# Squares folded on the vector engine, junk matmuls moved, and a conditioning pair loaded by half chunks, in the head of a decoder trunk

## The chip, the cores and the metric

The kernel runs on one NeuronCore of a Trainium2 chip. The metric is device time of one execution in microseconds, median over several; smaller is better. Five engines have queues of their own: TensorE (PE; its weight loads are shown as PEld), VectorE (DVE), ScalarE (ACT), GpSimd (POOL) and SyncE (SP), which issues almost all transfers.

## The reference, cut to what matters

Two layers over one sequence of 256 positions and 1024 channels, in float32. A layer is a token mixer and a squared-ReLU MLP; each is preceded by an RMSNorm that is modulated by a vector c:

```python
c_act = jax.nn.silu(c)
for i in range(DEPTH):
    mod = c_act @ w_mod[i] + b_mod[i]
    sh1, sc1, g1, sh2, sc2, g2 = jnp.split(mod, 6, axis=-1)
    h = modulate(rmsnorm(x, norm_mix[i]), sh1, sc1)     # h * (1 + sc1) + sh1
    y = pool_mixer(h, ...) if i % 2 == 0 else moba_attention(h, ...)
    x = x + g1[:, None, :] * y
    h = modulate(rmsnorm(x, norm_mlp[i]), sh2, sc2)
    x = x + g2[:, None, :] * squared_relu_mlp(h, w_up[i], w_down[i])
return rmsnorm(x, norm_final)
```

The change lies in layer 0, between the pooling mixer's output and the first matmul of the up projection.

## The kernel before

Activations lie channels by positions: `xs[k]` is block k of 128 channels (k from 0 to 7), 128x256. Weights stream in chunks of 1 MB, in the hand-written order `LOADS`, into five buffers (`RAW_BUFS`); `issue()` asks SP for the next chunk of the order each time a buffer's last use has been issued. Weights of the MLPs and projections are split into a high and a low part (ScalarE casts, L247; VectorE subtracts, L252), and each product takes three matmul passes.

The head of the program, up to about 54 us, is one order written out by hand. It computes six vectors of layer 0 as needed, each cut into four pieces of 256 channels. A "pair" is two such pieces whose weights (2 MB) come in two chunks. `pair_mm` (`take`, L313) multiplies c into one chunk, with 32 output columns in each of four quarters of the array, and `pair_out` (`given`, L324) picks each channel's value from the result and adds the bias, on VectorE. There are two layouts. Pairs in `BY_VECTOR` have a whole vector's piece in each chunk: a take is 64 passes of 64 columns, and each piece is finished after its own chunk. The other pairs have half of the summed dimension of both pieces in each chunk: a take is 32 passes of 128 columns, and both pieces are finished after the second chunk (`both_given`).

The mixer works in four groups of 256 channels, 3 to 0. `pool_out(g)` adds the gated mixer output to x (L453) for the group's two blocks, and ScalarE squares them (L528). `pool_sums` sums the squares over channels with matmuls whose moving operand is one column of ones (`sums`, L389: two matmuls of two passes each for one block). `n1.rstd()` makes the norm row r from the sums (one ScalarE step, then five on VectorE, L399 to L406), and `n1.spread()` (L410) multiplies it out to all partitions. The pair mlp0 is the scale and the shift of the MLP's norm for channels 0 to 255. `gain` (L357) joins the scale with the norm's weight. `Input.scaled` (L637) multiplies x by gain and norm on VectorE, `Input.high` (L643) adds the shift and rounds to the high part on ScalarE, `Input.low` (L646) makes the rest. Then `up` runs its 256 tiles; the first eight are done in three sweeps of eight matmuls (`mm_sums`, L279), later ones three passes at a time. The pair mlp1 is taken at tiles 13 and 20.

`keep_warm(n)` issues n matmuls of a constant tile (L342, "junk", two passes of 256 columns each) whose result nothing reads.

In the head before, mlp0's first take ran ahead of the spread and its second behind it:

```python
    take("mlp0", 0)
    given("mlp0", 0)
    ...
    R1 = n1.spread()
    take("mlp0", 1)
    ...
    first.scaled(R1)
    given("mlp0", 1)
```

Of the kernel before, what the change touches and what calls it, by code (L numbers as in the profile page):

```python
# [51 lines left out]
PAIRS |= {f"mlp{j}": ((0, 4, j), (0, 3, j)) for j in range(2)}  # L52
PAIRS["shift2"] = ((0, 3, 2),)

BY_VECTOR = {"g10", "mlp0", "shift2"}


G_UP0, G_UP1, G_QKV, G_WO = 14, 4, 4, 5
# [82 lines left out]
def tile_hybrid_pool_moba(  # L141
# [12 lines left out]
    nc = tc.nc  # L154
# [11 lines left out]
    def bank(name):  # L166
        return ps.tile([P, 512], F32, tag="ps", name=name)

    def al_tile(shape, name, dt=F32):
        return act.tile(shape, dt, tag="al", bufs=KF, name=name)  # L170
# [11 lines left out]
    def issue():  # L182
        i = n_issued[0]
        if i == len(LOADS):
            return
        n_issued[0] += 1
        key = LOADS[i]
        half = HALF * P
        if key[0] == "p":
            t = al_tile([P, 4 * P], f"wp{key[1]}")  # L190
            nc.sync.dma_start(t, w_pool[0][:, key[1] * 4 * P : (key[1] + 1) * 4 * P])
        elif key[0] == "w0a":
            t = loaded["w", 0] = raw_tile("w_0")
            nc.sync.dma_start(t[:, :half], w_all[0][:, :half])
        elif key[0] == "w0b":
            t = loaded["w", 0]
            nc.sync.dma_start(t[:, half:], w_all[0][:, half:])
        else:
            if key[0] == "c":
                layer, m, j = PAIRS[key[1]][key[2]]  # L200
                src = w_mod[layer, m * 4 + j]
            else:
                src = w_mod[key[1], key[2] * 4 + key[3]] if key[0] == "m" else w_all[key[1]]
            t = raw_tile("_".join(str(a) for a in key))
            nc.sync.dma_start(t, src)
        loaded[key] = t

        if n_issued[0] < len(LOADS) and LOADS[n_issued[0]][0] in ("p", "w0b"):
            issue()
# [7 lines left out]
    for _ in range(RAW_BUFS):  # L217
        issue()
    ident = vec[:, V_ID : V_ID + P]
    pick = vec[:, V_PICK : V_PICK + 32]  # L220
    rc = vec[:, V_RC : V_RC + 64].rearrange("p (a b) -> p a b", a=4)
    ones = const.tile([P, 1], F32, name="ones")
# [21 lines left out]
    def split_hi(h):  # L244
        raw = loaded["w", h // 2][:, h % 2 * HALF * P : (h % 2 + 1) * HALF * P]
        hi = split_p.tile([P, HALF * P], F32R, tag="whi", name=f"w{h}_hi")
        nc.scalar.copy(hi, raw)  # L247
        return raw, hi
# [56 lines left out]
    def pair_mm(name, i, region):  # L305
        whole = name in BY_VECTOR
        nk = KD if whole else KD // 2
        w = loaded["c", name, i].rearrange("p (k q n) -> p k q n", k=nk, q=4)
        cols = slice(64 * i, 64 * i + 64) if whole else slice(0, P)
        for k in range(nk):  # L310
            c0 = k if whole else i * nk + k
            for q in range(4):
                nc.tensor.matmul(  # L313
                    region[32 * q : 32 * q + 32, cols], ccol[:, c0 : c0 + 1].to_broadcast([P, 32]), w[:, k, q],
                    start=c0 == 0, stop=c0 == KD - 1, skip_group_check=True,
                )
        issue()

    def pair_out(name, i, region):
        key = PAIRS[name][i]  # L320
        layer, m, j = key
        for a in range(2):
            t = tmp.tile([P, 32], F32, tag="pk", bufs=4, name="pk")
            nc.vector.scalar_tensor_tensor(  # L324
                t, region[:, (2 * i + a) * 32 : (2 * i + a + 1) * 32], mod_bias(*key)[:, a : a + 1], pick,
                op0=ALU.add, op1=ALU.mult, accum_out=mods[layer, m][:, 2 * j + a : 2 * j + a + 1],
            )
        known.add(key)
# [11 lines left out]
    def keep_warm(n):  # L340
        for _ in range(n):
            nc.tensor.matmul(junk[0][:, :S], fill[:, :P], fill, start=True, stop=True)  # L342
# [23 lines left out]
    class Rms:  # L366
# [13 lines left out]
        def fold(self, k):  # L380
            if k > 0:
                nc.vector.tensor_add(self.acc, self.acc, self.sq.pop(k))
# [69 lines left out]
    def residual_sum(src, k, gate):  # L452
        nc.vector.scalar_tensor_tensor(xs[k], src, gate[:, k : k + 1], xs[k], op0=ALU.mult, op1=ALU.add)  # L453
# [65 lines left out]
    n1 = Rms("n1")  # L519
    sq1 = {}  # L520

    def pool_out(g):
        cols = slice(2 * g, 2 * g + 2)
        nc.vector.tensor_mul(g1[:, cols], mods[0, 2][:, cols], vec[:, V_PSC + 2 * g : V_PSC + 2 * g + 2])
        for n in range(2):
            residual_sum(pools[g][:, n * S : (n + 1) * S], 2 * g + n, g1)
            sq1[2 * g + n] = al_tile([P, S], f"n1_sq{2 * g + n}")
            nc.scalar.activation(sq1[2 * g + n], xs[2 * g + n], AF.Square)  # L528

    def pool_sums(g):  # L530
        for n in range(2):
            n1.sums(sq1[2 * g + n], (g, n) == (0, 1))

    def take(name, half):
        pair_mm(name, half, region[name])

    def given(name, i):
        pair_out(name, i, region[name])

    def both_given(name):  # L540
        for i in range(2):
            given(name, i)
# [55 lines left out]
    pool_products(0)  # L598
    both_given("g32")
    pool_out(3)  # L600
    pool_out(2)
    take("g10", 0)
    given("g10", 0)
    pool_out(1)
    pool_sums(3)
    pool_sums(2)
    take("g10", 1)
    given("g10", 1)
    pool_out(0)
    pool_sums(1)  # L610
    pool_sums(0)
    n1.rstd()
    take("mlp0", 0)
    given("mlp0", 0)
    gs01 = const.tile([P, KD], F32, name="gs0_4")
    gain(0, 4, V_NMLP, gs01, 0, 2)
    R1 = n1.spread()
    take("mlp0", 1)
    junk[0] = bank("junk2")
    keep_warm(2)  # L620

# [213 lines left out]

    first = Input(0)
    first.scaled(R1)
    given("mlp0", 1)
    w0 = split_hi(0)
    first.high()  # L840
    first.low(0)
# [172 lines left out]
    for i, (n, k) in enumerate(QKV_ORDER):  # L1014
        w = next_tile()
        p, j = divmod(n, 3)
# [149 lines left out]
```

## Time and profile before

| | |
|---|---|
| median of 3 executions | 549.41 us (549.16 to 550.0) |
| the profiled execution, its own time | 550.51 us |
| its span, first to last instruction | 548.7 us |
| mean granted TensorE clock | 0.990 |
| busy share: PE, PEld, DVE, ACT | 98%, 91%, 75%, 59% |
| moved by DMA | 140.43 MB, mean 256 GB/s |

All times in the rows are microseconds from the first instruction. The profiled execution's own time is the span and 1.8 us around it. An engine's busy time says little by itself; the chain that ended last says which work set the end, and the windows say in which stretch an engine was full. "issue" in the chain is time in which an engine waited for nothing that the profile shows.

### The profile page before, as it was taken

Reading aid. Unit: us, or ns where it says so; the run is one execution under the profiler, and the core shown is the slowest. Engines: PE = TensorE matmul, PEld = TensorE weight load, DVE = VectorE, ACT = ScalarE, POOL = GpSimd, SP = SyncE. Lnnn points to the kernel's source line nnn. Section 1 sums busy time; section 2 is a strip of 40 time slices with the busy share of each in tenths; the row PEclk is TensorE's granted clock in tenths of the full one; section 3 lists DMA queues with packets and bytes.
Section 4 is the critical chain, followed back from the end, with each engine's and each line's share of the span. In section 5 each row is a group of like instructions: output and inputs, shape, how many; then the busy total and the mean of one; then the engine's idle time right before and its main releaser. Section 6 shows DMA issues by size and latency. Waiting matters only on the chain.

```text
span 548.7 us, 11124 instructions
## 1 busy us (share of the span) xinstructions
PE 537.5 (98%) x4492; PEld 499.5 (91%) x4492; DVE 410.5 (75%) x830; ACT 323.6 (59%) x605; POOL 2.5 (0%) x18
## 2 busy tenths in 40 slices
PE   8998999999999999999999999999999999999995
PEld 7777999999988888999999899999999998888895
DVE  2865598799889889966999994777887786665541
ACT  4224335789744445546988778566997774444531
POOL 1000000000000000000000000000000000000000
PEclk9997999999999999999999999999999999999998
DMA  8999989468999988974558774353565567676002
GB/s 335 416 420 406 360 321 380 177 231 300 318 383 392 382 334 324 351 254 153 189 213 297 289 288 163 121 206 141 177 226 173 212 230 260 221 263 254 1 1 76
DMA packets 22339, 140.43 MB, mean 256 GB/s; under 512 B 2416, under 2 KB 4608, under 8 KB 5904
## 3 DMA queue, kind: packets, MB, share of 16 engines
q1 hardware_dynamic: 22048, 138.61, 67.8%
q10 hardware_dynamic: 144, 1.05, 0.5%
q8 instruction: 35, 0.57, 0.4%
q14 instruction: 16, 0.13, 0.1%
q0 software_dynamic: 96, 0.06, 0.0%
HBM read 138.64 MB, written 1.07 MB: 255 GB/s over the span
## 4 chain that ended last, share of the span: by engine, by line
PE 92%; DMA 6%; DVE 0%; issue 0%; ACT 0%; DVEq 0%; ACTq 0%
PE m1d L264 9%; PE m0d L264 9%; PE m1u L271 6%; PE m1u L272 6%; PE m1u L273 6%; PE m0u L271 5%; PE m0u L273 5%; PE m0u L272 5%; PE m1d L265 5%; PE m0d L265 5%; PE qkv L271 5%; PE qkv L272 4%; PE qkv L273 4%; DMA raw_c_sh<-in_w_mod 3%; DMA raw_c_g<-in_w_mod 2%; PE wo L271 1%
## 5 line engine op out<-in xcount | busy, mean ns | idle before, releaser
L252 DVE TENSOR_TENSOR w_lo<-raw_w,w_hi 128x1024 fp32r<-128x1024 f32 x160 | 194.6, 1223 | 59.5 <-ACT w_hi L247 57.8
L247 ACT CAST w_hi<-raw_w 128x1024 fp32r<-128x1024 f32 x160 | 166.4, 1047 | 76.6 <-PE m1d L264 25.0
L264 PE MATMUL m1d<-m1u_al,w_hi 128*128 128x512 f32 x224 | 78.7, 394 | 0.0
L264 PE MATMUL m0d<-m0u_al,w_hi 128*128 128x512 f32 x224 | 78.1, 392 | 0.0
L295 DVE SCALAR_TENSOR_TENSOR raw_m<-raw_m,cact 128x1024 f32<-128x1024 f32 x62 | 75.3, 1218 | 0.0
L271 PE MATMUL m1u<-h_raw,w_hi 128*128 128x258 f32 x256 | 72.8, 284 | 0.0
L272 PE MATMUL m1u<-h_raw,w_hi 128*128 128x256 f32 x256 | 72.6, 284 | 0.0
L273 PE MATMUL m1u<-h_raw,w_lo 128*128 128x258 f32 x256 | 72.5, 283 | 0.0
L271 PE MATMUL m0u<-h,w_hi 128*128 128x256 f32 x248 | 69.8, 282 | 0.0
L273 PE MATMUL m0u<-h,w_lo 128*128 128x256 f32 x248 | 69.7, 281 | 0.0
L272 PE MATMUL m0u<-h,w_hi 128*128 128x256 f32 x248 | 69.4, 280 | 0.0
L265 PE MATMUL m1d<-m1u_al,w_lo 128*128 128x256 f32 x224 | 63.0, 281 | 0.0
L265 PE MATMUL m0d<-m0u_al,w_lo 128*128 128x256 f32 x224 | 62.8, 280 | 0.0
L271 PE MATMUL qkv<-h_raw,w_hi 128*128 128x258 f32 x192 | 57.4, 299 | 0.0
L272 PE MATMUL qkv<-h_raw,w_hi 128*128 128x256 f32 x192 | 54.6, 284 | 0.0
L273 PE MATMUL qkv<-h_raw,w_lo 128*128 128x258 f32 x192 | 54.4, 283 | 0.0
L264 PEld LDWEIGHTS m1d<-m1u_al,w_hi 128*128 128x128 f32 x224 | 42.1, 188 | 9.9
L264 PEld LDWEIGHTS m0d<-m0u_al,w_hi 128*128 128x128 f32 x224 | 42.1, 188 | 9.5
L273 PEld LDWEIGHTS m1u<-h_raw,w_lo 128*128 128x128 f32 x256 | 48.8, 191 | 0.0
L271 PEld LDWEIGHTS m1u<-h_raw,w_hi 128*128 128x128 f32 x256 | 48.7, 190 | 0.0
L272 PEld LDWEIGHTS m1u<-h_raw,w_hi 128*128 128x128 f32 x256 | 48.5, 190 | 0.0
L271 PEld LDWEIGHTS m0u<-h,w_hi 128*128 128x128 f32 x248 | 46.7, 188 | 0.9 <-issue 0.8
(179 smaller groups left out, 993.2 us busy)
## 6 DMA issues: line engine op xcount, KB each, us to landing
raw_w<-in_w_all SPq DMA_DIRECT2D x79, 1024.0 KB, 6.5
raw_m<-in_w_mod SPq DMA_DIRECT2D x31, 1024.0 KB, 6.8
raw_c_sh<-in_w_mod SPq DMA_DIRECT2D x8, 1024.0 KB, 13.6
raw_c_g<-in_w_mod SPq DMA_DIRECT2D x4, 1024.0 KB, 12.7
raw_c_mlp<-in_w_mod SPq DMA_DIRECT2D x4, 1024.0 KB, 10.7
T<-bd SPq DMA_DIRECT2D x8, 256.0 KB, 10.3
x<-in_xT ACTq DMA_DIRECT2D x1, 1024.0 KB, 5.9
wp<-in_w_pool SPq DMA_DIRECT2D x4, 256.0 KB, 14.1
```

The lines of the kernel that those rows point to most:

```text
L247: nc.scalar.copy(hi, raw)
L252: nc.vector.tensor_sub(lo, raw, hi.bitcast(F32))
L264: nc.tensor.matmul(b, hi, hl[:, : 2 * S], start=start, stop=False)
L265: nc.tensor.matmul(b[:, S:], lo, hl[:, :S], start=False, stop=stop)
L271: nc.tensor.matmul(dst, hi, xh, start=start, stop=False)
L272: nc.tensor.matmul(dst[:, :S], hi, xl, start=False, stop=False)
L273: nc.tensor.matmul(dst, lo, xh, start=False, stop=stop)
L295: nc.vector.scalar_tensor_tensor(raw[:, a], raw[:, a], 1.0, cact, op0=ALU.mult, op1=ALU.mult, accum_out=dst[:, a : a + 1])
```

## The change

The squares of groups 3 and 2 are added on VectorE into one block (7 += 6, 5 += 4, 7 += 5), which is summed by one `sums` call; the squares of blocks 3, 2, 1 and 0 keep calls of their own. Within a group the second block is treated first. Sums that stood between the two g10 takes stand behind the second one, and junk calls are placed between takes and sums. The pair mlp0 leaves `BY_VECTOR`, so its chunks are laid out as halves of both pieces; both takes stand ahead of the spread, and both pieces are picked ahead of the gain.

```diff
-BY_VECTOR = {"g10", "mlp0", "shift2"}
+BY_VECTOR = {"g10", "shift2"}
...
     def pool_out(g):
         cols = slice(2 * g, 2 * g + 2)
         nc.vector.tensor_mul(g1[:, cols], mods[0, 2][:, cols], vec[:, V_PSC + 2 * g : V_PSC + 2 * g + 2])
-        for n in range(2):
+        for n in (1, 0):
             residual_sum(pools[g][:, n * S : (n + 1) * S], 2 * g + n, g1)
...
-    def pool_sums(g):
-        for n in range(2):
-            n1.sums(sq1[2 * g + n], (g, n) == (0, 1))
+    def pool_sum(k):
+        n1.sums(sq1[k], k == 0)
+
+    def fold(k, j):
+        nc.vector.tensor_add(sq1[k], sq1[k], sq1[j])
...
     pool_out(3)
     pool_out(2)
+    fold(7, 6)
+    fold(5, 4)
+    fold(7, 5)
     take("g10", 0)
+    keep_warm(2)
     given("g10", 0)
     pool_out(1)
-    pool_sums(3)
-    pool_sums(2)
     take("g10", 1)
     given("g10", 1)
     pool_out(0)
-    pool_sums(1)
-    pool_sums(0)
+    pool_sum(7)
+    keep_warm(1)
+    pool_sum(3)
+    pool_sum(2)
+    keep_warm(1)
+    pool_sum(1)
+    pool_sum(0)
     n1.rstd()
+    keep_warm(1)
     take("mlp0", 0)
-    given("mlp0", 0)
+    take("mlp0", 1)
+    both_given("mlp0")
     gs01 = const.tile([P, KD], F32, name="gs0_4")
     gain(0, 4, V_NMLP, gs01, 0, 2)
     R1 = n1.spread()
-    take("mlp0", 1)
     junk[0] = bank("junk2")
     keep_warm(2)
...
     first = Input(0)
     first.scaled(R1)
-    given("mlp0", 1)
     w0 = split_hi(0)
     first.high()
```

## Rows read from the trace of the kernel before

**Rows 1.** Windows: stretch, its length, busy time (instructions) of each engine, clock, transfer share.

```profile
54.00:140.00 86.00, 86.00 (x824) 84.38 (x823) 72.33 (x126) 53.53 (x99) 0.00 (x0) 1.00 0.80 299
```

**Rows 2.** The chain that ended last, 38 to 54 us: start, length, what.

```profile
40.09 1.88 PE n_rms L389 x16
...
44.78 1.87 PE n_rms L389 x8
...
48.92 1.15 PE n_rms L410 x4
...
51.73 1.51 issue
53.23 0.70 PE junk L342 x2
```

**Rows 3.** Windows of four stretches of the head.

```profile
39.50:43.00 3.50, 3.50 (x117) 3.25 (x105) 1.79 (x8) 1.50 (x4) 0.00 (x0) 1.00 1.01 419
43.00:50.00 7.00, 6.84 (x85) 6.10 (x85) 2.77 (x17) 2.12 (x4) 0.00 (x0) 0.51 1.02 417
39.54:47.05 7.51, 7.35 (x134) 6.80 (x127) 3.29 (x16) 2.55 (x7) 0.00 (x0) 0.74 1.01 412
47.05:53.20 6.15, 4.67 (x128) 3.78 (x127) 3.73 (x18) 2.79 (x5) 0.00 (x0) 0.77 1.03 410
```

**Rows 4.** The page: busy time by engine, and the instruction queue (packets, MB, share).

```profile
PE 537.5 (98%) x4492; PEld 499.5 (91%) x4492; DVE 410.5 (75%) x830; ACT 323.6 (59%) x605; POOL 2.5 (0%) x18
...
q8 instruction: 35, 0.57, 0.4%
```

**Rows 5.** DMA queues in 37.0:37.1, in 44.48:44.55 and in 50.77:50.85, in this order.

```profile
q8 instruction: 1, 0.02, 66.8%
...
q8 instruction: 1, 0.02, 98.9%
...
q8 instruction: 1, 0.02, 85.9%
```

**Rows 6.** Groups by line and shape, VectorE: count, busy us, mean ns, idle before.

```profile
L382 DVE TENSOR_TENSOR n_acc<-n_acc,n_sq 128x256 f32<-128x256 f32 x12 | 5.0, 419 | 0.0
```

**Rows 7.** Timeline of TensorE, 27 to 31 us: start, length, instructions merged (count).

```profile
27.89 1.08 PE L313 MATMUL pma<-raw_c_sh,ccol 128*32 128x128 f32 x32
28.91 1.13 PE L342 MATMUL junk<-fill 128*128 128x256 f32 x4
```

**Rows 8.** Timeline, 36 to 54 us, in brackets the idle time before and its releaser.

```profile
37.09 0.25 DVE L324 SCALAR_TENSOR_TENSOR pk<-pmb,vec 128x32 f32<-128x32 f32 x1 [1.93 <-PE pmb L313]
...
37.78 0.15 DVE L524 TENSOR_TENSOR g1p<-mod,vec 128x2 f32<-128x2 f32 x1
...
43.73 0.88 DVE L453 SCALAR_TENSOR_TENSOR x<-pool,g1p,x 128x256 f32<-128x256 f32 x2
44.31 0.81 ACT L528 ACTIVATE n_sq<-x 128x256 f32<-128x256 f32 x2 [2.16 <-DVE x L453]
...
46.57 2.35 PE L313 MATMUL pmb<-raw_c_mlp,ccol 128*32 128x64 f32 x64
...
47.06 1.62 PEld L313 LDWEIGHTS pmb<-raw_c_mlp,ccol 128*32 128x32 f32 x57 [0.29 <-issue]
...
50.00 1.10 PE L313 MATMUL pmb<-raw_c_mlp,ccol 128*32 128x64 f32 x64
...
50.10 0.87 DVE L637 SCALAR_TENSOR_TENSOR h_u<-x,gs,n_rms 128x256 f32<-128x256 f32 x2 [0.52 <-PE n_rms L410]
...
51.46 0.91 ACT L643 ACTIVATE h<-h_u,mod 128x256 fp32r<-128x256 f32 x2 [3.27 <-DVE pk L324]
...
53.58 0.59 PE L279 MATMUL m0u<-h,w_hi 128*128 128x256 f32 x2
```

**Rows 9.** Tile raw_c_mlp: landing of the transfers issued at 31.4 and at 34.7.

```profile
DMA to landing us min/median/max: 11.9/11.9/11.9
...
DMA to landing us min/median/max: 11.2/11.2/11.2
```

## The prediction

> **What bounds the kernel now.** The page's first part has TensorE busy for 98% of the span [rows 4], and the windows say where that is without a gap: from 54 to 140 us, the up projection of layer 0 almost to its end, it is busy all the time at full clock, with the transfer engines at 0.80 of theirs [rows 1]. The change doesn't touch those stages, but they slide: what the first tile of the projection wins comes off the end, unless a wait opens there. So the sum is the start of that tile, now 53.58 [rows 8].
>
> The chain of waits before it shows three troubles. First, one-column sums: sixteen passes of 1.88 us from 40.09, and the last eight behind the last square, 44.78 to 46.65 [rows 2]. Second, the clock: 1.00 in 39.5:43 and 0.51 in 43:50, so nearly all of that stretch ran at the lower level, 1.2 of 2.4 GHz [rows 3]. Before the fall, in 39.5:43, TensorE was busy throughout, but with 64-column takes and one-column sums alone.
>
> Third, two stops of TensorE that nothing in the profile releases: 0.29 us before 47.06, in the middle of a take whose data are there, and 1.51 us from 51.73, between two junk passes that wait for nothing [rows 2, 8]. I read them as late instructions. The page has 35 packets of 16 KB on the instruction queue q8, for 4492 matmuls and 4492 weight loads: 257 instructions a packet [rows 4]. From one stop to the next TensorE ran 128 matmuls and 127 loads, one packet's worth [rows 3]. A packet starts by 44.55 and one by 50.85 [rows 5]; each stop ends 2.5 us after its packet's start (47.06 - 44.5, 53.23 - 50.8). A third starts by 37.1, and from 39.54, 2.5 us on, to 47.05 TensorE again ran 127 loads [rows 3, 5]. So a block is entered at 39.54, the next one's packet starts 5.0 us later; entered at 47.06, the next starts 3.7 us later. The transfer engines are full there, 1.03 [rows 3].
>
> The Trainium skill (Runtime: NRT & Kernel Launch, section Instruction fetch mechanics) also has blocks of 16 KiB, 256 instructions, fetched while the one before is executed, but calls the cost of a crossing mostly hidden. The row of 1.51 us idle disagrees. By that rule no stop would be left in the new order either, which is rival (a).
>
> **The squares.** A fold is a 128x256 add like the norm's later ones, 0.42 us each [rows 6]; three in a row with starts some 0.35 apart are about 1.05 of VectorE ahead of the first g10 picks. The second g10 take moves ahead of sixteen sum passes (1.88) and behind four junk passes (about 0.93, from 1.13 less the last pass's tail [rows 7]): 0.95 earlier. If none of the folds were hidden, the last square would end 1.05 later than 44.31 + 0.81 = 45.12; if all were, 0.95 earlier [rows 8]. I take 44.65: the folds keep VectorE half a microsecond behind the earlier take. The order 1, 0 inside a group costs nothing, as both members are one instruction of one size.
>
> TensorE keeps 20 sum passes of 32, at 1.88 / 16 = 0.117 us each at full clock [rows 2]. Sum 7 follows the second g10 take, sums 3 and 2 and two junk calls fill the wait, and sums 1 and 0 stand behind the squares: the last ends at 45.25, where it now ends at 46.65.
>
> Does the clock hold? Junk of 256 columns now comes at most 1.5 us apart, where 3.5 us of sums and takes without any fell. I take full clock; half clock, the other bound, is priced below.
>
> **The mlp0 pair.** A take becomes 32 passes of 128 columns, 1.08 us [rows 7], for 64 of 64 columns, 1.10 at full clock and 2.35 at half [rows 8]. Both chunks are there: landed at 31.4 + 11.9 = 43.3 and 34.7 + 11.2 = 45.9 [rows 9]. The instructions may not be. From 39.54, where nothing differs yet, 128 pairs on is nine pairs into the first mlp0 take: 24 pairs left of the first g10 take, 4 junk, 64 of the second, 20 sums, 6 junk, which is 118, and one further instruction of a wait. TensorE gets there at 46.0 (45.25, a junk call of 0.47, nine pairs). Its packet was asked for before the change begins, so I keep its arrival: 47.06. A stop of 1.05 us thus stands where 1.4 us of sums went, and folds and junk are worth nothing beyond it; even with the folds wholly unhidden TensorE would come to this place at about 47. Behind it: 23 pairs (0.73) to 47.8, the second half to 48.85, the spread row, which took 1.15 at half clock [rows 2] and takes about 0.7 here, to 49.65. The norm's r is no limit: it needed under 2.3 us from the last sum to the spread (46.65 to 48.92, a take between), and has 3.6.
>
> VectorE: four picks 0.69 (37.09 to 37.78), the gain 0.19, then the scaled rows [rows 8]. Picks at 48.95, gain 49.65, scaled 49.83, where it was 50.10. Now two of those picks stand behind the scaled rows, and ScalarE's high half waits for them until 51.46 [rows 8]; after, nothing stands between. From a VectorE row's start to ScalarE's next one is 0.58 (43.73 to 44.31), so the high half starts at 50.4. That is 1.06 earlier. The cast queued ahead of it on ScalarE is over in both orders: ScalarE idles 3.27 us before 51.46 [rows 8]. SP: the buffers of g10 and mlp0 come free about 1 us earlier and the mlp1 transfers are issued so much earlier, into a stream that is full: no gain, no loss.
>
> The next block begins 128 pairs after 47.06: 55 of the takes, 8 of spread and junk, 24 of the projection's first eight tiles, 15 of the next five, so it begins inside the first mlp1 take, due near 56.4. Its packet needs what it needed, 6.2 us, to 53.2. So the stop of 1.51 us goes; what hides the packet is the slower run of the first thirteen tiles. The first tile starts when its high half is there, 50.4 + 0.53 = 50.93; the four junk passes are over at 50.6. The low half and the low weights (VectorE, to 52.6) come before the passes that want them.
>
> **The sum.** High half 51.46 to 50.4: -1.06. From high half to first tile 2.12 (51.46 to 53.58), now 0.53: -1.59. Together -2.65. The profiled span of 548.7 becomes 546.05; that execution took 550.51, 1.8 more than its span and 1.1 above the median of 549.41. On the median: 546.8.
>
> **Rivals.** (a) The packet is earlier or the crossing is hidden: no stop at 46.0, all behind it 1.05 earlier, -3.7, 545.7. For it: fewer instructions in all; against: the request lies ahead of the change. The section of the Trainium skill named above would have this one. (b) The packet is 1.2 later (the two ways from entry to packet differ by that), or the clock falls while TensorE stands there: 55 pairs at half clock cost some 1.8 more. Then -1.45 or -0.85: 548.0 to 548.6. For it: idle behind thin sums; against: the stop of 1.51 us didn't lower the clock. (c) The clock falls at 43 as now: sums to 47.3, takes at half clock to 52.2, high half 53.8, and the gain is gone: 549.4. The same comes of data that arrive late in the projection; the share of 0.80 speaks against that [rows 1]. (d) Slower: the clock falls so and rises only behind the first tiles: the start 0.7 late, and their first 2.4 us of tiles doubled: +2, 551.4 or so. It decides from where the low stretch outlasts 54; now it ends at 50, lifted by takes that are to be shorter.
>
> **How the numbers follow.** Forecast 0.55, (a) 0.12, (b) 0.15, (c) 0.13, (d) 0.05. A range of 545.5 to 548.7 leaves out (c) and (d). 0.2%, 1.1 us, is about what a measurement of this kernel can tell from no change: faster by more are the forecast, (a) and over half of (b), 0.76; slower 0.05; the rest 0.19.
>
> **What would show it.** First tile near 51.0; clock 1.00 in 43:50; an idle of about 1 us inside the first mlp0 take that ends near 47; none between the last junk passes; the high half 0.6 after the first scaled row. I am wrong if the clock falls, if the stop is longer or elsewhere, or if TensorE waits in the projection.

## The result, and the profile after

| | before | after |
|---|---|---|
| median of 7 executions each | 550.0 us | 546.96 us |
| profiled execution, its own time | 550.51 | 547.1 |
| its span | 548.7 | 545.3 |
| high half on ScalarE starts | 51.46 | 50.36 |
| first tile of the up projection starts | 53.58 | 50.92 |

The ratio of the times is 0.995 with a 95% interval of 0.9936 to 0.9965, so 2.75 us less, between 1.9 and 3.5; the medians are 3.04 apart. The forecast was 546.8, with the first tile at 50.93.

Windows of the kernel after: length, busy time (instructions) of PE, PEld, DVE, ACT and POOL, clock, transfer share, GB/s. They answer [rows 1, 3].

```profile
39.50:43.00 3.50, 3.07 (x118) 2.36 (x106) 3.12 (x13) 1.24 (x4) 0.00 (x0) 1.00 1.00 418
43.00:46.50 3.50, 3.50 (x26) 3.08 (x25) 1.51 (x9) 1.33 (x4) 0.00 (x0) 1.00 1.01 406
46.50:50.00 3.50, 3.42 (x73) 2.83 (x72) 1.59 (x15) 1.04 (x1) 0.00 (x0) 1.00 1.03 428
...
54.00:140.00 86.00, 86.00 (x824) 84.37 (x823) 73.87 (x130) 54.48 (x102) 0.49 (x1) 1.00 0.82 311
```

The clock holds 1.00 where it was 0.51. From 54 to 140 us TensorE is as full as before, so nothing in that stretch gave the head's gain back.

The chain that ended last, kernel after, 40 to 54 us: start, length, what. It answers [rows 2].

```profile
40.94 0.42 DVE n_sq L535
41.36 0.35 DVE pk L325 x4
...
41.76 1.10 PE pmb L314 x64
...
45.26 0.79 PE n_rms L390 x8
46.05 0.54 PE junk L343 x2
46.59 0.45 PE pmb L314 x9
47.03 0.08 issue
47.11 1.77 PE pmb L314 x55
...
48.90 0.77 DVE pk L325 x8
...
49.84 0.49 DVE h_u L648
...
50.36 0.52 ACT h L654
...
50.92 3.13 PE m0u L280 x24
```

Eight sum passes behind the last squares take 0.79 us where eight took 1.87. The mlp0 takes break after nine passes. From the last take the chain leaves TensorE and goes through VectorE and ScalarE, one step behind the other, to the first tile. The 1.51 us of "issue" are gone. New at its head is a path that before had not shown: folds, picks of the first g10 half, and only then the second g10 take.

The timeline of the kernel after, with the idle time ahead of an instruction and its releaser in brackets, says the same of the two waits. It answers [rows 8].

```profile
40.48 0.88 DVE L535 TENSOR_TENSOR n_sq<-n_sq,n_sq 128x256 f32<-128x256 f32 x2 [0.15 <-ACT n_sq L529]
41.28 0.24 DVE L325 SCALAR_TENSOR_TENSOR pk<-pmb,vec 128x32 f32<-128x32 f32 x1
...
41.76 0.94 PEld L314 LDWEIGHTS pmb<-raw_c_g,ccol 128*32 128x32 f32 x64 [0.83 <-DVE pk L325]
...
46.51 0.25 PEld L314 LDWEIGHTS pmb<-raw_c_mlp,ccol 128*32 128x32 f32 x9 [0.33 <-issue]
...
47.10 1.46 PEld L314 LDWEIGHTS pmb<-raw_c_mlp,ccol 128*32 128x32 f32 x55 [0.34 <-issue]
...
49.21 0.73 PEld L343 LDWEIGHTS junk<-fill 128*128 128x128 f32 x4
```

The four junk weight loads at 49.21 run through without a stop; the two junk matmuls of before were parted by one. The queue of instructions has a packet that starts by 44.75 and the next one by 50.95 (the first row is the window 44.68:44.75, the second 50.88:50.95 of the kernel after), as in [rows 5]:

```profile
q8 instruction: 1, 0.02, 96.8%
...
q8 instruction: 1, 0.02, 95.4%
```

The stop that ends at 47.10 ends 2.4 us after the start of the first, near the 2.5 of before.

**How the span's 3.41 us divide.** The first tile is 2.66 earlier. The first and last matmuls of the two down projections lie 0.13 and 0.54 closer together than before: 89.20 for 89.33 and 89.35 for 89.89, taken from the trace to the hundredth. That leaves about 0.1. The prediction had no term for the 0.67 of the down projections, which the change does not touch.

### The profile page after: what moved, and what is told of

It reads as the page before. It is cut to its first block, busy times and chain, and to the rows that moved or that the text cites. A ratio compares the mean times of both kernels' runs of the same rounds, so it can differ in the third digit from the quotient of the medians.

```text
span 545.3 us, 10993 instructions
## 1 busy us (share of the span) xinstructions
PE 534.0 (98%) x4426; PEld 495.9 (91%) x4426; DVE 411.2 (75%) x833; ACT 323.7 (59%) x605; POOL 2.5 (0%) x18
## 3 DMA queue, kind: packets, MB, share of 16 engines
q10 hardware_dynamic: 144, 1.05, 0.5%
## 4 chain that ended last, share of the span: by engine, by line
PE 91%; DMA 6%; DVE 1%; ACT 0%; issue 0%; DVEq 0%; ACTq 0%
PE m1d L265 9%; PE m0d L265 9%; PE m1u L272 6%; PE m1u L273 6%; PE m1u L274 6%; PE m0u L272 5%; PE m0u L274 5%; PE m0u L273 5%; PE m0d L266 5%; PE m1d L266 5%; PE qkv L272 5%; PE qkv L273 4%; PE qkv L274 4%; DMA raw_c_sh<-in_w_mod 3%; DMA raw_c_g<-in_w_mod 2%; PE wo L272 1%
```

## The experiments

The change has three parts: the folds with the new order of sums, the added junk, and the mlp0 pair. The table collects the profiles with each combination (second profiles are e11 and e12 below). The clock is that of the window 47:51 us of each run. The ratios are to executions of the kernel before that were taken along with each run; their medians were 549.63 (e1, e2, e3, e5), 549.96 (e4, e6, e7) and 549.9 (e8, e9, e10).

| folds | junk | pair | run | first tile | clock 47:51 | median | ratio to before |
|---|---|---|---|---|---|---|---|
| no | no | no | before, second profile | 53.81 | 0.50 | | |
| no | no | yes | e1 | 52.53 | 0.50 | 549.22 | 0.9989 [0.998, 0.9999] |
| no | yes | no | e7 | 53.27 | 0.64 | 549.71 | 0.9998 [0.9987, 1.0009] |
| yes | no | no | e10 | 52.55 | 0.50 | 548.37 | 0.9972 [0.9961, 0.9983] |
| yes | yes | no | e2 | 52.82 | 0.57 | 549.17 | 0.9982 [0.9968, 0.9995] |
| yes | no | yes | e3 | 51.84 | 0.69 | 547.94 | 0.9962 [0.9948, 0.9976] |
| no | yes | yes | e4 | 54.13 | 0.50 | 551.14 | 1.0015 [1.0002, 1.0027] |
| yes | yes | yes | after, second profile | 51.01 | 1.00 | | |

Each first tile and clock is that of one profiled execution. In the rows with folds 0.67 us of the time, 0.0012 of the ratio, is not the head's: it is the placement of buffers, which e8 and e9 show.

### One part alone: e1, e7, e10

e1, the pair alone, on the kernel before:

```diff
-BY_VECTOR = {"g10", "mlp0", "shift2"}
+BY_VECTOR = {"g10", "shift2"}
...
     take("mlp0", 0)
-    given("mlp0", 0)
+    take("mlp0", 1)
+    both_given("mlp0")
...
     R1 = n1.spread()
-    take("mlp0", 1)
...
-    given("mlp0", 1)
     w0 = split_hi(0)
```

> The kernel before, with the pair mlp0 alone changed (half chunks, both takes and all four picks ahead of the spread row); squares, sums and junk as before. Packet theory (the gain is the high half freed of the late picks, and the instruction stop of 1.51 us moved into the projection, where it is hidden): the clock falls at 43 as before, the sums end at 46.65, the instructions of the take come at 47.06, and the 56 pairs left at half clock end near 50.4. Then picks 50.5, scaled rows 51.4, high half 51.9, first tile 52.5 without a stop in front: 1.1 us faster than before. Clock theory (the gain is the clock that stays up, so sums and takes run at full speed): the clock falls here, so at most 0.3 us faster.

Measured: the first tile at 52.53, the high half at 51.97. The gap between the two is 0.56, so in this execution 1.56 of the 2.12 is gone, the term of the prediction. But the two takes now stand in the half-clock stretch ahead of the spread, and push the high half 0.5 back. The first tile is where the packet theory had it, 52.5. The time does not choose between the theories: the ratio gives 0.6 us less than before (0.1 to 1.1), the medians 0.4, where 1.1 and at most 0.3 were forecast.

e7, the junk alone, on the kernel before:

```diff
     take("g10", 0)
+    keep_warm(2)
...
     pool_sums(2)
+    keep_warm(1)
...
     pool_out(0)
+    keep_warm(1)
     pool_sums(1)
     pool_sums(0)
     n1.rstd()
+    keep_warm(1)
     take("mlp0", 0)
```

> The kernel before with the added junk calls alone, at the like places (behind the first g10 take, ahead of the second, ahead of the last sums, behind the norm row); no folds, pair mlp0 as before. Clock theory: the clock stays at its upper level and sums and the first mlp0 take run in half the time, 1.4 us or more faster than before. Packet theory: the clock stays up, but sums and first take end where they did (junk is added, the take's instructions come near 47), and the junk behind the second mlp0 take still stands for a block of instructions until about 53: first tile 53.2 to 54, within 0.4 us of before.

Measured: no difference (549.71 against 549.96 for the kernel before). The junk kept the clock at 1.00 through 43:47, and in 47:51 it was 0.64. The last sums ended at 47.39, where they ended at 46.65, since junk now stands ahead of them. Alone it gives back what it wins. The first tile, 53.27, is within the packet theory's range, but not by its path: the stop near 53 is not there, as the packet started at 49.68.

e10, the folds with the new order of sums, alone; the folds as in the change, and behind them:

```diff
     take("g10", 0)
     given("g10", 0)
     pool_out(1)
-    pool_sums(3)
-    pool_sums(2)
     take("g10", 1)
     given("g10", 1)
     pool_out(0)
-    pool_sums(1)
-    pool_sums(0)
+    pool_sum(7)
+    pool_sum(3)
+    pool_sum(2)
+    pool_sum(1)
+    pool_sum(0)
```

> The kernel before with the folds and the new order of sums, without the added junk and with the mlp0 pair in its old layout and place. Theory (folds pay only together with the pair, since with the old pair the two instruction stops and the picks behind the scaled rows set the first tile): first tile between 52.5 and 53.6 whether the clock falls or not, placement as in the changed kernel (89.20 and 89.35), so 0.7 to 1.7 us less than before. Rival (the folds alone hold the clock through the head and take the sums off the path): high half at 51.0 or earlier, first tile at 51.5 or earlier, 2.7 us or more less than before.

Measured: first tile 52.55, inside 52.5 to 53.6, and 1.5 us less than before by the medians, so the theory held. The high half started at 51.76, behind the picks of 51.46; the rival wanted 51.0. The clock fell (0.80 in 43:47), and a stop of 0.64 us, 2.4 behind its packet, stood in the first mlp0 take after 19 pairs.

### One part undone: e2, e3, e4

e2, the kernel after with the mlp0 pair as it was before:

```diff
-BY_VECTOR = {"g10", "shift2"}
+BY_VECTOR = {"g10", "mlp0", "shift2"}
...
-    take("mlp0", 1)
-    both_given("mlp0")
+    given("mlp0", 0)
...
     R1 = n1.spread()
+    take("mlp0", 1)
...
     first.scaled(R1)
+    given("mlp0", 1)
```

> The changed kernel with the pair mlp0 back in its old layout and place; folds, order of sums and junk as changed. Packet theory: the clock stays up, the first stop ends at 47.1 inside the first mlp0 take, the scaled rows start near 49.0 and the high half near 50.5; but 128 pairs on is again the junk behind the second take, so TensorE stops there until about 53.2 and the first tile starts at 53.4: 0.2 to 0.3 us faster than before. Clock theory: first tile half a microsecond behind the high half, near 51.0, and 2.5 us faster than before.

Measured: high half 52.19, first tile 52.82. The chain of e2, where the clock fell during the stop (1.00 in 47.25:47.5, 0.50 from 47.75):

```profile
46.74 0.28 PE pmb L314 x9
47.02 0.72 issue
47.74 1.72 PE pmb L314 x55
```

The stop is in the same place, after nine passes, and longer: its packet started at 45.24, 0.53 later than in the kernel after, and the stop ended 2.50 behind it. Counted from the last weight load, as in the timeline, it is 0.88 for 0.34. Neither forecast came true. The packet theory wanted a second stop and the first tile at 53.4, but the next packet started at 50.36, just in time; the clock theory wanted 51.0, but the clock fell. The times of e2 lay in two groups, near 549.2 and at 547.6 to 548.1, with one more at 551.1; the profile is of the upper group. The mean clocks, 0.994 to 0.996 in both groups, do not part them, and what does stays open.

e3, the kernel after without its added junk:

```diff
     take("g10", 0)
-    keep_warm(2)
...
     pool_sum(7)
-    keep_warm(1)
     pool_sum(3)
     pool_sum(2)
-    keep_warm(1)
     pool_sum(1)
     pool_sum(0)
     n1.rstd()
-    keep_warm(1)
     take("mlp0", 0)
```

> The changed kernel without the four added junk calls (the one behind the first g10 take, the two between the sums, the one behind the norm row). If the junk is what holds the clock: it falls near 43 to the lower level for some 7 us, sums end near 46.0 and the second half of the mlp0 pair near 50.2, first tile near 52.3, 1.4 us slower than the changed kernel. If fewer one-column sums hold it by themselves: full clock, first tile within 0.1 of 50.9, no difference from the changed kernel, since the take waits for its instructions until 47.1 either way.

Measured: the clock fell, only at about 46, and the first tile came at 51.84, 0.92 behind the kernel after; the median is 1.0 above it. The forecast had the fall near 43. So the junk does hold the clock in the kernel after, for about 1 us.

e4, the kernel after without folds, so with 12 more one-column passes:

```diff
-    fold(7, 6)
-    fold(5, 4)
-    fold(7, 5)
...
-    pool_sum(7)
+    for k in (7, 6, 5, 4):
+        pool_sum(k)
     keep_warm(1)
```

> The changed kernel without the three folds; the squares of blocks 7, 6, 5 and 4 have sums of their own where the folded block had one (12 passes more). If the folds are worth little: VectorE takes the first g10 picks at 40.3 and not at 41.3, so the second g10 take starts near 41.1 for 41.76, and the longer sums end near 46.9 for 46.05; the instructions of the mlp0 take are there by then (47.1), the takes run 47.4 to 49.4, first tile 51.5: 0.5 us slower than the changed kernel. If the sums' passes are what the change saves (12 passes of 0.117 on the path): 1.4 us slower.

Measured: 551.14, 4.2 us more than the kernel after, and more than the kernel before. Both forecasts were too small. The chain of e4:

```profile
44.53 0.79 PE n_rms L390 x8
45.31 0.59 PE junk L343 x2
45.90 1.50 PE n_rms L390 x8
47.40 1.06 PE junk L343 x2
48.46 3.62 PE pmb L314 x64
...
53.57 0.52 ACT h L652
...
54.13 1.94 PE m0u L280 x14
```

Two groups of eight passes stand there, 0.79 and 1.50 us: the clock fell between them. The junk after it takes 1.06 for 0.54, the mlp0 takes 3.62 for some 2.2. First tile 3.2 later; the down projections are back at 89.33 and 89.89, another 0.67. That is the 3.9 between the two profiled executions (550.99 and 547.1); the other 0.3 is how these lie to their medians. The 12 passes themselves are only 12 x 0.117 = 1.4 us. So the folds are worth more than their passes: in these profiles, only kernels with all three parts kept the clock at 1.00 through 47:51. The mean clocks of e4's other executions agree. Eleven of the twelve had 0.991 to 0.994 and took 549.7 to 551.5; one had 0.997 and took 548.2. So without folds most of the 4.2 seems to go with the clock, which falls in most executions and not in all; no profile of that one is kept.

### Where the packets stand: e5, e11, e12

e5, the kernel after with 24 more pairs of instructions early in the program and the same work in them:

```diff
-    keep_warm(13)
+    keep_warm(1)
+    for _ in range(24):
+        nc.tensor.matmul(junk[0][:, :P], fill[:, :P], fill[:, :P], start=True, stop=True)
```

> The changed kernel with 24 of the junk passes at the very start cut in two of half the width: 24 pairs of instructions more, the same columns, in a stretch where TensorE waits for its first data until 9.1 us. Packet theory: every block of instructions begins 24 pairs earlier in the code, so the stop at 46.8 leaves the mlp0 take and falls three passes before the end of the sums of squares 3 and 2; TensorE stands from about 44.4 until about 47.1, everything behind comes 2.6 us later, first tile 53.5, and the gain of the change is gone (2.6 us slower than the changed kernel). If the stops are waits for something in the code (a bank, a semaphore): they stay in the mlp0 take and the time is that of the changed kernel.

Measured: 547.43, first tile 51.37. The chain of e5:

```profile
44.59 0.45 PE n_rms L390 x5
45.03 0.10 issue
45.13 0.39 PE n_rms L390 x3
```

Counted back 24 pairs from nine passes into the mlp0 take (nine, two of junk, eight sums, two of junk, three sums), this is the place to the instruction, so the stops are the boundaries of the blocks. The price was wrong: the packets came earlier as well, at 32.92 and 42.69 where after had 37.34 and 44.71, and the stop, which again ended 2.4 us after its packet's start, was 0.10. Of e5's twelve executions seven took 546.9 to 547.6 at mean clocks of 0.997 to 0.999, and five 548.4 to 550.0 at 0.990 to 0.995. No profile of those five is kept, so where their clock was low is not shown; but that all three parts hold it in every execution is not shown either.

e11 and e12 are the kernels before and after, unchanged, in one more execution each.

> The kernel before, unchanged, in another execution. Theory (the instruction packets of the head do not start at the same time in every execution, and so the two stops before are not of one length): the second stop, 1.51 us before 53.23 in the profile of before, differs by 0.5 us or more, and the first tile of the projection with it, while the down projections take 89.33 and 89.89 again. Each stop still ends 2.4 to 2.6 us after its packet's start. Rival (they are set by the program): both stops within 0.2 us of 0.29 and 1.51, first tile within 0.3 of 53.58.

> The changed kernel, unchanged, in another execution. Theory (as for the other run): the stop inside the first mlp0 take differs from 0.3 us or is gone, with the first tile within 0.5 of 50.92, since the packet is nearly in time; the down projections take 89.20 and 89.35. Rival: stop within 0.1 of 0.3, first tile within 0.1 of 50.92.

Measured: in e11 the second stop is 0.96, the first 0.20, and the first tile is at 53.81, within the 0.3 of the rival. The rows are of its chain:

```profile
51.87 0.63 PE junk L342 x2
52.50 0.96 issue
53.46 0.70 PE junk L342 x2
```

Its packets started at 44.70 and 50.98; the stops ended 2.6 and 2.5 us behind them. In e12 the packet started at 43.40, the take of mlp0 ran its 64 passes without a stop, and the first tile was at 51.01:

```profile
47.03 1.93 PE pmb L314 x64
```

So the length of a stop belongs to the execution, and its place to the program. The first tile of e11 was not earlier for the shorter stop: TensorE came to the boundary 0.77 later, for the most part since its second mlp0 take ran 1.64 us, partly at the lower clock, instead of 1.10, and the packet came 0.2 later. What set the tile there is the packet, not TensorE's arrival. e12's second g10 take started at 42.20, 0.44 later than in the first profile of after, and its first tile only 0.09 later: the stop of 0.3 was worth about 0.35.

### Where the 0.67 us of the down projections come from: e8, e9

In the profiles above every kernel with folds has the two spans at 89.20 and 89.35, every one without at 89.33 and 89.89, whatever its head did. The buffers of the squares are used again for the hidden vector. With folds they come free in another order, and in the compiled program three of its 32 tiles in each layer change places. e8 is the kernel before with the squares summed in another order:

```diff
-    pool_sums(3)
-    pool_sums(2)
+    for k in (7, 5, 4, 6):
+        n1.sums(sq1[k], False)
```

> The kernel before with one thing changed: the four squares of groups 3 and 2 are summed in the order 7, 5, 4, 6 where it was 6, 7, 4, 5. Passes, operands' shapes and everything around them are the same. The buffers of the four squares come free in another order, and in the compiled program three tiles of the hidden vector of each layer change places with one another, to just where the changed kernel has them. Theory (placement alone): the down projection of layer 0 takes 89.20 from its first to its last matmul's start instead of 89.33, that of layer 1 89.35 instead of 89.89, the first tile of the up projection stays within 0.4 of 53.58, and the time is 0.67 us less than before. Rival (the gain at the end of the program comes of the head, for instance of work that lies earlier against the transfers): 89.33 and 89.89 stay, and the time is that of before.

e9 is the kernel after with the folds as a chain:

```diff
-    fold(7, 6)
-    fold(5, 4)
-    fold(7, 5)
+    fold(6, 7)
+    fold(5, 6)
+    fold(4, 5)
...
-    pool_sum(7)
+    pool_sum(4)
```

> The changed kernel with the three folds as a chain (6 += 7, 5 += 6, 4 += 5, then block 4 is summed) in place of a tree (7 += 6, 5 += 4, 7 += 5). Buffers then come free in the order in which the kernel before freed them, and the tiles of the hidden vector lie as they lay before. Theory (placement alone): the two down projections take 89.33 and 89.89 again, so 0.67 us more than the changed kernel has. In the head one fold less stands behind the last square of the two groups, so that the second g10 take starts up to 0.4 earlier than 41.76, and the stop inside the first mlp0 take, which ends when its instructions are there, takes that up: first tile within 0.2 of 50.92. In all 0.67 slower than the changed kernel, some 2.0 faster than before. Rival: the down projections keep 89.20 and 89.35, and the time is that of the changed kernel within 0.3.

Measured: e8 has 89.20 and 89.35, e9 has 89.33 and 89.89. The tile view of the down projection of layer 1, two lines of each kernel: count, duration in ns (least, median, most), first and last start. Before, after, e8, e9:

```profile
L264 PE MATMUL m1d<-m1u_al,w_hi x224: 388/394/403, 449.7 to 528.0; 128*128 128x512 f32 x112
...
L273 PE MATMUL m1d<-m1u_al,w_lo x32: 276/280/287, 528.6 to 539.6; 128*128 128x256 f32 x32
```

```profile
L265 PE MATMUL m1d<-m1u_al,w_hi x224: 388/393/403, 446.8 to 524.6; 128*128 128x512 f32 x112
...
L274 PE MATMUL m1d<-m1u_al,w_lo x32: 276/279/283, 525.2 to 536.1; 128*128 128x256 f32 x32
```

```profile
L264 PE MATMUL m1d<-m1u_al,w_hi x224: 388/393/403, 448.2 to 526.0; 128*128 128x512 f32 x112
...
L273 PE MATMUL m1d<-m1u_al,w_lo x32: 276/279/283, 526.6 to 537.6; 128*128 128x256 f32 x32
```

```profile
L265 PE MATMUL m1d<-m1u_al,w_hi x224: 388/394/403, 447.1 to 525.4; 128*128 128x512 f32 x112
...
L274 PE MATMUL m1d<-m1u_al,w_lo x32: 276/280/287, 526.0 to 537.0; 128*128 128x256 f32 x32
```

Same instructions, same shapes, same clock; a nanosecond in the median decides. Since e8 changes only an order and the old places come back in e9, the placement is the cause. Why those addresses are slower was not tried.

The times are 548.69 for e8, 0.9984 [0.9974, 0.9994] of before, and 547.94 for e9, 0.9965 [0.9951, 0.9979]. In e8 the head missed its forecast: first tile 52.31 instead of 53.58, with packets at 43.34 and 49.51 and a second stop of 0.30 that ended 2.39 us behind. In e9 the second g10 take started at 41.71, only 0.05 earlier: the chained folds run back to back behind the squares and end no sooner. The first tile was 0.40 earlier than after's because the packet, at 42.65, left no stop, which is outside the forecast 0.2; the projection then ran 0.5 us longer than after's. Half of that comes at 86.2, where a weight load waits 0.17 us for the low weights from VectorE; the rest comes bit by bit up to 96 us, with no idle time in the profile, and why stays open.

### A version that beats both: e6

e6 takes the hidden wait of the second g10 take away: g10 also by half chunks, so that nothing is picked between its takes, and the first mlp0 take moved under the squares.

```diff
-BY_VECTOR = {"g10", "shift2"}
+BY_VECTOR = {"shift2"}
...
-    given("g10", 0)
-    pool_out(1)
     take("g10", 1)
-    given("g10", 1)
+    both_given("g10")
+    pool_out(1)
     pool_out(0)
     pool_sum(7)
     keep_warm(1)
+    take("mlp0", 0)
     pool_sum(3)
     pool_sum(2)
-    keep_warm(1)
     pool_sum(1)
     pool_sum(0)
     n1.rstd()
-    keep_warm(1)
-    take("mlp0", 0)
     take("mlp0", 1)
```

> The changed kernel with the pair g10 by half chunks too, its four picks together behind the second take; the first mlp0 take ahead of the sums of squares 3 and 2, the second behind the norm row; without the last two added junk calls. 64 pairs of instructions fewer ahead of the mlp0 takes: if the packet theory holds, the block that the changed kernel waits for until 47.1 now begins in the projection's first sweep, so nothing waits for it. Picks of g10 at 42.1, last residual 44.9, sums end near 46.4, second mlp0 take to 47.4, picks to 48.2, scaled rows 48.5, high half 49.1, first tile 49.6: 1.3 us faster than the changed kernel, if the clock holds (if it falls as it did without junk, the two are level).

Measured: 545.89, 0.9927 [0.9913, 0.9941] of before and by the medians 1.1 us less than after, whose interval, 0.9936 to 0.9965, it just touches. The chain of e6:

```profile
43.41 1.08 PE pmb L314 x32
44.49 1.89 PE n_rms L390 x16
...
46.41 0.27 ACT n_s L398
...
47.36 0.16 DVE n_r L407
47.52 0.70 DVE pk L325 x8
...
48.91 0.52 ACT h L651
...
49.47 1.58 PE m0u L280 x11
```

No stop is left, and the norm row with its six small steps now sets the first tile, 0.1 from the forecast. Several things change at once here, and which of them gives how much was not tried.

## Why the prediction was right, point by point

**The pair, right.** The high half moved by -1.10 for -1.06, the gap to the first tile went from 2.12 to 0.56 for 0.53. Scaled rows started at 49.84 for 49.83. The two terms are not equally the pair's own. The gap is the second stop, and it closes in other ways too: to 0.56 in e1, but also to 0.63 in e2, with the old pair, where the packet came just in time, and to 0.56 in e8 with a packet at 49.51. In e11 it was 1.57. What the pair alone gives is a high half that waits for no picks behind the scaled rows. From the first scaled row to the high half it is 0.51 to 0.52 us in all eight profiles with the new pair, where the prediction said 0.58, and 1.36 to 2.19 in the six with the old one, whatever clock and packets did. With the clock held as well, the high half came 1.10 earlier; with the clock fallen, in e1, it came 0.51 later than before.

**The place of the stop, right; its size not.** Nine pairs into the first mlp0 take was exact, and e5 moved it by 24 pairs as counted. The stop was forecast at 1.05 us and measured 0.3. The term that failed is TensorE's arrival, 46.0: it came at 46.76 (46.51 + 0.25). Behind that stands the second g10 take, which was to move 0.95 earlier, from 41.90 to about 40.95; it started at 41.76. Missed was a wait: the take writes into the bank of PSUM from which VectorE still picks the first half, and the folds stand ahead of these picks. The three folds took VectorE from 39.91 to 41.36, 1.45 us with a wait for ScalarE's squares, and not the 1.05 of the prediction. The row at 41.76 names the picks as releaser, and e4, without folds, started this take 0.7 earlier. The last sums so ended at 46.05, not 45.25.

**Why the sum held all the same.** The stop took up the difference, as the prediction said it would for folds that were not hidden, and the packet came at 44.71, as at 44.5 before. That was partly luck: in e12 it came at 43.40. With a packet in time rival (a) gave 3.7 us; e12 gave the same first tile to 0.1, because TensorE was late as well.

**"Folds and junk are worth nothing beyond it", the stop, failed.** It held for the microseconds of the passes, and not for the clock. The prediction took full clock as given and asked what the stop left. e3 lost 0.92 at the first tile and e4 3.2, both with the clock falling. Rival (c), the clock as before, is what e4 comes to, with the high half at 53.57 for 53.8; in e3, where it fell 3 us later, a third of the head's gain went. That rival was priced too low: its own working puts the first tile at 54.3, which is 0.75 later than before and 550.2, not 549.4. Rival (d) has the same kind of slip, as its two parts, 0.7 and 2.4, make 3.1 and not 2. The kernel after had 1.00 in all its windows from 39.5 to 54.

**The second boundary, right.** The 1.51 us stop is gone; the next packet started by 50.95, and 54 to 140 us shows no idle.

**What was not in the sum.** The 0.67 us of placement. By spans, -2.66 of the head, -0.67 and a rest of -0.08 make the -3.41. Of medians the same would be 550.0 - 2.65 - 0.67 = 546.7, and 546.96 was measured. The forecast of 546.8 stood on a median of 549.41, at the low side of later ones (549.63 to 550.0), and lacked the 0.67: two errors that nearly cancelled. Rival (d) had no support: TensorE was at full clock when the first tiles came.

## What to carry to other kernels

Price a reordered head by what each engine waits for in program order, picks of a shared bank included, and not only by the work moved: an addition on VectorE, hidden by count, delayed a matmul through the picks behind it. Count instructions as well as microseconds where TensorE runs many short ones, because a stop stands at a place that can be counted, while its length must be kept as a range. Where two kernels differ by less than a microsecond, compare stages that neither change touches first; the allocation of buffers may account for it.

## What the runs showed of the hardware that was not expected

**Instruction packets.** In the fourteen profiles eleven stops are seen at a block boundary of the head. All ended 2.4 to 2.6 us after the start of their packet on q8 (for example 47.10 - 44.71, 47.74 - 45.24, 45.13 - 42.69, 53.46 - 50.98), with the transfer share at 1.0. The eleventh, 0.23 us in e1, ended at 39.65, 2.6 behind the packet of 37.05, with 24 pairs of the first g10 take to go: this is the boundary from which the prediction counts. The Trainium skill (Runtime: NRT & Kernel Launch, section Instruction fetch mechanics) calls the crossing mostly hidden; in this head it cost from nothing (e12) to 1.51 us, and for one program it differed by half a microsecond between executions.

**The clock beside full activity.** In e4 TensorE had no idle time in 43:47 and the mean granted clock there was 0.83, then 0.50 in 47:51, with one-column sums and junk in the stretch. The first of these windows, of e4:

```profile
43.00:47.00 4.00, 4.00 (x28) 3.90 (x29) 0.72 (x2) 0.81 (x2) 0.00 (x0) 0.83 1.01 407
```

**Placement.** The same 544 matmuls of m1d took 89.35 or 89.89 us from first to last start according to where three of 32 input tiles lay.
